# A new issue order for the output projection and the experts of a diffusion block; all normed rows stay on chip for the router

## The chip, the cores and the metric

The kernel runs on one core of a Trainium2 chip. The metric is the device time of one execution in microseconds; a time is told as the median of several executions. Durations and waits come from one profiled execution.

## The reference

One layer of a diffusion block, 1024 latent tokens and 256 context tokens of width 1024, all in float32:

```python
h = rmsnorm(x, g_mix[l]) * (1.0 + sc1) + sh1
hc = rmsnorm(xc, g_mix[l]) * (1.0 + csc1) + csh1
y, y_c = token_mixers(h, hc, w_in[l], w_out[l], ...)     # three head groups, then concat @ w_out
x = x + gt1 * y
h2 = rmsnorm(x, g_ffn[l]) * (1.0 + sc2) + sh2
x = x + gt2 * hier_moe(h2, w_rg[l], b_rg[l], w_re[l], b_re[l], w_gate[l], w_up[l], w_down[l])
...
return rmsnorm(x, g_final)

def hier_moe(h, ...):        # 4 groups of 4 experts: best group, best 2 experts in it
    ...
    for e in range(N_EXPERTS):
        he = jax.nn.silu(t @ w_gate[e]) * (t @ w_up[e])
        y = y + gates[:, e:e + 1] * (he @ w_down[e]).astype(jnp.float32)
```

There are 16 experts with matrices of 1024 x 512, 1024 x 512 and 512 x 1024.

## The kernel before, in words

Up to about 590 us the kernel computes the input projections and the three head groups. The change leaves that part as it is. What follows, the output projection, the router, the experts and the last norm, is one list of steps (`Plan`), each with its engine, a planned duration, what it reads and writes, and a sort key. A list scheduler goes through a model of the engines and queues and takes, among the steps that are ready, the one of smallest key, where `SHIFT2` adds a number to the key of each kind of step. `emit` then issues the instructions in that order, and each engine works through its own in that order. So the tables of numbers decide the order on every engine, and the instructions themselves stay the same. An instruction that waits holds up all that stands behind it on its engine.

Precision: every float32 weight slab of 128 x 512 (256 KB) is split into a high and a low part. `slab` issues the load on SP (L1029) into one of seven places (the names R, late_vcB, kv and kc), ACT writes the high part (L1049), and DVE, for some slabs POOL, writes the low part (L1026) into a ring of 31 places (W, WX and late_ names). A product on PE is three matmuls of 512 columns (L1062, L1063, L1064).

The output projection goes over eight tiles of 128 tokens with 16 products each, 128 in all. Behind the two halves of a tile stand on DVE the gated residual (L1145, L1147), then the norm (L1163) and the shift (L1166). The normed rows go to DRAM (h2d, L1167), from where the experts gather them. The router of a tile transposes the normed rows (L1068, step `ot`), forms the logits of 4 groups and 16 experts (L1184, `ol`), finds group, two experts, gates and slots in some thirty small steps on DVE (from L1191 on: groups, choose from L1203 on, base L1221, gates, slots), and writes two entries for each token into a table in DRAM by an indirect DMA of POOL (L1247). For the tiles named in `AGAIN` the transposes read the normed rows from a copy that SP reads back from h2d (L1029 into a tile F), in place of the rows that DVE has written:

```python
H2 = Hn
if t in AGAIN:
    H2 = ("F", "h2", t)
    k += LAGR
    load(1.39, (k, "hr"), lambda: buf(H2), lambda: h2d[rows], [H2], r=[("h2d", t)],
         after=[chain["lg", t - 1]] if t else [])
```

A matmul with ones (L1281) counts the tokens of each expert three times: over the first two tiles (it names the first expert), over the first six (`rank_experts`, L1296 to L1308, orders the others by their count, into `oi`), and over all eight. The 16 experts, in the order of their count, are worked through in 23 blocks (numbers 0 to 22) of 128 or 64 table rows. The first expert has block 0 (128 rows) and 1 (64), which hold tokens of tiles 0 to 5 alone, and block 2, which needs all tiles. Blocks 20, 21 and 22 are those of the last three experts, block 3 that of the second. For a block SP loads the table's rows (L1426 into IX), POOL gathers the tokens (L1429), PE transposes them into one of two buffers T (L1444), ACT takes the high part (L1456) and DVE the low one (L1460); such a buffer is free when both have read it. Then come 8 gate, 8 up and 8 down products, and POOL adds the result, times a gate (L1491), to the sum in DRAM (L1432). The last expert's block takes the sum back itself (L1568) and writes its rows of the output, beside the last norm of all tiles (`final_tile`, from L1588 on). The 15 experts behind the first bring 15 x 24 = 360 slabs.

## Time and profile before

| | |
|---|---|
| median of 3 executions | 1187.8 us (1187.21 to 1189.05) |
| profiled execution | 1187.43 us |
| its span in the trace | 1185.7 us |
| mean granted clock of PE, as a share of full speed | 0.953 |
| PE busy | 1051.8 us (89%) |
| DVE busy | 914.1 us (77%) |
| ACT busy | 723.3 us (61%) |
| POOL busy | 415.5 us (35%) |
| read from and written to DRAM | 168.95 MB and 24.07 MB |

PE is TensorE, DVE VectorE, ACT ScalarE, POOL GpSimd; SP is the engine that issues most transfers. Busy time leaves out the issuing of DMAs. The execution took 1.7 us more than the span of its trace.

### The profile page before, as it was taken

Reading aid. Unit: us, or ns where it says so; the run is one execution under the profiler, and the core shown is the slowest. Engines: PE = TensorE matmul, PEld = TensorE weight load, DVE = VectorE, ACT = ScalarE, POOL = GpSimd, SP = SyncE. Lnnn points to the kernel's source line nnn. Section 1 sums busy time; section 2 is a strip of 40 time slices with the busy share of each in tenths; the row PEclk is TensorE's granted clock in tenths of the full one; section 3 lists DMA queues with packets and bytes.
Section 4 is the critical chain, followed back from the end, with each engine's and each line's share of the span. In section 5 each row is a group of like instructions: output and inputs, shape, how many; then the busy total and the mean of one; then the engine's idle time right before and its main releaser. Section 6 shows DMA issues by size and latency. Waiting matters only on the chain. (4 is left out here: it accounts for less than half of the span.)

```text
span 1185.7 us, 18611 instructions
## 1 busy us (share of the span) xinstructions
PE 1051.8 (89%) x5620; PEld 834.4 (70%) x5620; DVE 914.1 (77%) x1742; ACT 723.3 (61%) x1451; POOL 415.5 (35%) x451
## 2 busy tenths in 40 slices
PE   5899999987999999999889986898999999999680
PEld 1688677766888888888667875676767767676560
DVE  6765779747788787788667778879787878888875
ACT  7774122218888988888732332377676667667763
POOL 0200000102778687876613444312212313222220
PEclk9899999998999999999989896799999999999895
DMA  8624674010000000000054673589999999899995
GB/s 309 228 86 145 201 234 153 10 38 11 19 1 19 1 2 19 10 1 11 13 186 150 194 225 122 163 268 280 273 295 283 293 288 285 254 284 283 277 319 226
DMA packets 99980, 191.30 MB, mean 161 GB/s; under 512 B 17720, under 2 KB 19560, under 8 KB 99750
## 3 DMA queue, kind: packets, MB, share of 16 engines
q1 hardware_dynamic: 93606, 172.59, 44.0%
q0 software_dynamic: 6272, 17.51, 6.6%
q8 instruction: 45, 0.74, 0.3%
q14 instruction: 57, 0.47, 0.1%
HBM read 168.95 MB, written 24.07 MB: 163 GB/s over the span
## 5 line engine op out<-in xcount | busy, mean ns | idle before, releaser
L685 DVE TENSOR_REDUCE st<-SC 128x1 f32<-128x1280 f32 x64 | 95.2, 1487 | 21.2 <-PE SC L680 16.3
L417 PE MATMUL acc<-wh,hH 128*128 128x512 f32 x256 | 101.3, 397 | 2.7 <-ACT bu L517 1.4
L418 PE MATMUL acc<-wl,hH 128*128 128x512 f32 x256 | 101.6, 398 | 0.0
L419 PE MATMUL acc<-wh,hL 128*128 128x512 f32 x256 | 100.8, 394 | 0.0
L1062 PE MATMUL A<-W,XP 128*128 128x512 f32 x236 | 98.3, 416 | 0.0
L1063 PE MATMUL A<-W,XP 128*128 128x512 f32 x236 | 95.4, 404 | 1.6 <-DVE W L1026 1.6
L688 ACT ACTIVATE P<-SC,st 128x1280 f32<-128x1280 f32 x64 | 85.1, 1330 | 17.0 <-DVE st L685 15.8
L1064 PE MATMUL A<-W,XP 128*128 128x512 f32 x236 | 95.0, 403 | 0.0
L1049 ACT ACTIVATE W<-R 128x512 fp32r<-128x512 f32 x111 | 68.9, 626 | 27.3 <-DMA R<-in_w_out_dram 6.4
L1026 DVE TENSOR_TENSOR W<-R,W 128x512 fp32r<-128x512 f32 x102 | 69.3, 690 | 17.9 <-ACT W L1049 15.9
L620 ACT ACTIVATE PT<-T 128x512 f32<-128x512 f32 (+1 forms) x126 | 65.1, 545 | 11.4 <-PE T L616 8.0
L732 PE MATMUL T<-vc,PT 128*128 128x64 f32 x512 | 62.2, 275 | 0.3
L1432 POOL DMA_INDIRECT accd<-F,IX x18 | 30.6, 1700 | 89.2 <-DVE F L1491 35.8
L732 PEld LDWEIGHTS T<-vc,PT 128*128 128x128 f32 x512 | 59.7, 192 | 0.7 <-ACT PT L620 0.4
L417 PEld LDWEIGHTS acc<-wh,hH 128*128 128x128 f32 x256 | 48.4, 189 | 14.2 <-issue 2.5
L680 PE MATMUL SC<-KC,QC 128*128 128x512 f32 (+1 forms) x192 | 52.4, 381 | 6.7 <-ACT P L688 6.3
L419 PEld LDWEIGHTS acc<-wh,hL 128*128 128x128 f32 x256 | 48.5, 189 | 11.4 <-issue 1.0
L418 PEld LDWEIGHTS acc<-wl,hH 128*128 128x128 f32 x256 | 48.4, 189 | 10.5 <-issue 0.7
L844 DVE TENSOR_REDUCE ast<-SA 128x1 f32<-128x640 f32 (+1 forms) x64 | 50.2, 785 | 6.5 <-PE SA L837 5.8
L442 DVE SCALAR_TENSOR_TENSOR macc<-mw,cs,macc 128x512 f32<-128x512 f32 x56 | 41.8, 747 | 17.2 <-DMA mw<-in_w_ada_dram 16.6
L1063 PEld LDWEIGHTS A<-W,XP 128*128 128x128 f32 x236 | 46.1, 195 | 11.6 <-DVE W L1026 2.4
L1062 PEld LDWEIGHTS A<-W,XP 128*128 128x128 f32 x236 | 45.9, 194 | 11.2 <-ACT W L1049 0.3
(768 smaller groups left out, 3165.4 us busy)
## 6 DMA issues: line engine op xcount, KB each, us to landing
R<-in_w_gate_dram SPq DMA_DIRECT2D x74, 256.0 KB
R<-in_w_down_dram SPq DMA_DIRECT2D x73, 256.0 KB
R<-in_w_up_dram SPq DMA_DIRECT2D x72, 256.0 KB
mw<-in_w_ada_dram SPq DMA_DIRECT2D x64, 256.0 KB
wr<-in_w_in_dram SPq DMA_DIRECT2D x32, 256.0 KB
kc<-in_w_up_dram SPq DMA_DIRECT2D x20, 256.0 KB
kc<-in_w_down_dram SPq DMA_DIRECT2D x19, 256.0 KB
late_vcB<-in_w_gate_dram SPq DMA_DIRECT2D x18, 256.0 KB
```

Source lines behind the costliest of these rows:

```text
L417: nc.tensor.matmul(acc[:, n0:n1], lhsT=a, rhs=W[k][0][:, n0:n1], start=(k == 0), stop=False)
L418: nc.tensor.matmul(acc[:, n0:n1], lhsT=a, rhs=W[k][1][:, n0:n1], start=False, stop=False)
L419: nc.tensor.matmul(acc[:, n0:n1], lhsT=b, rhs=W[k][0][:, n0:n1], start=False, stop=(k == KD - 1))
L620: nc.scalar.activation(dst, src, AF.Copy)
L685: nc.vector.tensor_reduce(small[0][:, j:j + 1], buf(("SC", u, j))[:, 0:1280], axis=AX.X, op=OP.max, negate=True)
L688: nc.scalar.activation(buf(("P%d" % j, u)), buf(("SC", u, j))[:, 0:1280], AF.Exp, bias=small[0][:, j:j + 1], accum_out=small[0][:, 2 + j:3 ...
L732: nc.tensor.matmul(buf(O)[:, 0:64], lhsT=buf(("PT", u, g))[:, (c - c0) * 128:(c - c0 + 1) * 128], rhs=vc[c // 8][:, c % 8, h * 64:(h + 1) ...
L1026: (nc.gpsimd if engine == "POOL" else nc.vector).tensor_sub(dst, a, b)
L1049: h = add("ACT", 0.525, (key, "sh"), lambda: nc.scalar.activation(buf(value)[:, 0:512], raw(), AF.Copy), r=r, w=[value], after=[chain["spl ...
L1062: nc.tensor.matmul(acc, lhsT=ah, rhs=w[:, 0:512], start=first, stop=False)
L1063: nc.tensor.matmul(acc, lhsT=ah, rhs=w[:, 512:1024], start=False, stop=False)
L1064: nc.tensor.matmul(acc, lhsT=al, rhs=w[:, 0:512], start=False, stop=last)
```

## The change

`AGAIN` is empty, so the transposes of tiles 0, 3 and 4 read the rows that DVE wrote, and three loads of 512 KB go. All shifts of the scheduler and their weight are new, and its planned durations are a little longer for products, transposes and slab loads and shorter for gathers and scatters. The number of matmuls is the same. The diff, cut to its core:

```diff
-SHIFT2 = dict(weight=0.005541, c=-100.3, fa=-315.5, fh=20.8, fl=78.4, fn=-1857.9, fo=545.6, fr=-845.7, fs=276.2,
+SHIFT2 = dict(weight=0.002103, c=-8803.8, fa=2162.2, fh=30.9, fl=130.5, fn=-2704.5, fo=-2557.1, fr=-4246.9, fs=742.6,
...
-AGAIN, LAGR = (0, 3, 4), 8.8
+AGAIN, LAGR = (), 8.8
...
-            chain["load"] = load(0.685, (key, "ld"), lambda: buf(R), src, [R], r,
+            chain["load"] = load(0.77, (key, "ld"), lambda: buf(R), src, [R], r,
...
-                    add("PE", 0.684, (b + 5.2 * n + 0.65 * k, "o"), lambda n=n, k=k, acc=acc: three(
+                    add("PE", 0.7, (b + 5.2 * n + 0.65 * k, "o"), lambda n=n, k=k, acc=acc: three(
...
-                add("PE", 0.36, (k, "ot"), ...
+                add("PE", 0.4, (k, "ot"), ...
...
-                ... w=[XG], dma=(m * 0.0164, 2.6, 2.1),
+                ... w=[XG], dma=(m * 0.0156, 2.6, 2.1),
...
-            us = 0.456 if half else 0.684
+            us = 0.466 if half else 0.7
...
-                    ... w=["sum"], dma=(m * 0.0258, 2.6, 2.7))
+                    ... w=["sum"], dma=(m * 0.0234, 2.6, 2.7))
```

What the order does at three places, as the programs have it. First, PE around the end of the output projection. Before, the last product of the projection is followed by the transposes (L1068) and logits (L1184) of tiles 6 and 7 and by the places of tile 5 (L1225, L1226), and the weights for the count over six tiles (L1281) are loaded behind them:

```order
L1064 MATMUL A_5685<-W_5684,XP_5666 128x512
L1068 MATMUL T_5692<-ident,F_5653 128x128 x4
L1068 MATMUL T_5691<-ident,F_5653 128x128 x4
L1225 LDWEIGHTS tri
L1225 MATMUL A_5687<-sel,tri 128x16
L1226 LDWEIGHTS ones
L1226 MATMUL A_5687<-sel,ones 128x16
L1184 MATMUL A_5688<-wr,kc 128x20 x8
L1068 MATMUL T_5692<-ident,F_5654 128x128 x4
L1068 MATMUL T_5691<-ident,F_5654 128x128 x4
L1184 MATMUL A_5690<-wr,kc 128x20 x8
L1281 LDWEIGHTS ones
```

After, the same count stands between two projection products (W are weight slabs, XP the token tile's two parts, A the accumulators):

```order
L1062 MATMUL A_5686<-W_5677,XP_5666 128x512
L1063 MATMUL A_5686<-W_5677,XP_5666 128x512
L1064 MATMUL A_5686<-W_5677,XP_5666 128x512
L1281 LDWEIGHTS ones
L1281 MATMUL A_5689<-selb,ones 128x16
L1225 LDWEIGHTS tri
L1225 MATMUL A_5687<-sel,tri 128x16
L1226 LDWEIGHTS ones
L1226 MATMUL A_5687<-sel,ones 128x16
L1062 MATMUL A_5690<-W_5672,XP_5666 128x512
L1063 MATMUL A_5690<-W_5672,XP_5666 128x512
```

From there 12 of the 128 projection products are still to come, of which this piece shows the first; before, all 128 stood ahead of the count. On DVE the ranking moves with it, ahead of the residual of tile 7; the low part for block 0 (L1460) now stands behind the small steps of tiles 6 and 7.

Second, SP's index loads. Before, nine of them (IX, L1426) follow the first nine slab loads of the second expert (the first rows here are the last two of these); five slab loads, eight index loads, and later the last four come behind them:

```order
L1029 ISA
L1029 DMA R_5663<-in_w_gate_dram 128x512
L1029 ISA
L1029 DMA kc<-in_w_up_dram 128x512
L1426 ISA
L1426 DMA IX_5631<-table 128x2
L1426 ISA
L1426 DMA IX_5632<-table 128x2
L1405 TENSOR_LOAD oi
L1426 ISA
L1426 DMA IX_5633<-table 64x2
L1405 TENSOR_LOAD oi
```

After, ten slab loads of that expert lie ahead, the first two of them ahead of block 0's index load, and all 21 index loads of blocks 2 to 22 follow one another before the second expert's third up slab:

```order
L1029 DMA R_5663<-in_w_gate_dram 128x512
L1029 ISA
L1029 DMA late_vcB<-in_w_up_dram 128x512
L1029 ISA
L1029 DMA R_5662<-in_w_up_dram 128x512
L1426 ISA
L1426 DMA IX_5631<-table 128x2
L1426 ISA
L1426 DMA IX_5632<-table 128x2
L1405 TENSOR_LOAD oi
L1426 ISA
L1426 DMA IX_5633<-table 64x2
```

Third, DVE near the end. Before, the low half of block 21's second transposes (XP<-T, L1460) stands behind 28 splits (L1026), the last five of them of gate slabs of block 21's own expert (late_yc<-late_vcB is the first), and a gate product (L1491):

```order
L1026 TENSOR_TENSOR late_yc<-late_vcB,late_yc 128x512
L1026 TENSOR_TENSOR WX_5657<-R_5661,WX_5657 128x512
L1026 TENSOR_TENSOR W_5670<-R_5660,W_5670 128x512
L1026 TENSOR_TENSOR late_bu<-R_5663,late_bu 128x512
L1026 TENSOR_TENSOR W_5679<-kc,W_5679 128x512
L1491 TENSOR_TENSOR F_5656<-A_5686,C_5664 128x512
L1460 TENSOR_TENSOR XP_5666<-T_5691,XP_5666 128x512
L1026 TENSOR_TENSOR late_shared<-R_5662,late_shared 128x512
```

After, both halves of block 21 stand close together, among splits of the gate slabs of the expert ahead, which is block 20's:

```order
L1026 TENSOR_TENSOR late_shared<-late_vcB,late_shared 128x512
L1026 TENSOR_TENSOR late_qc<-kc,late_qc 128x512
L1460 TENSOR_TENSOR XP_5666<-T_5691,XP_5666 128x512
L1488 SCALAR_TENSOR_TENSOR he_5668<-A_5687,IX_5648,he_5668 128x512
L1460 TENSOR_TENSOR XP_5666<-T_5692,XP_5666 128x512
L1026 TENSOR_TENSOR W_5672<-R_5663,W_5672 128x512
L1460 TENSOR_TENSOR late_qc<-T_5691,late_qc 128x512
L1026 TENSOR_TENSOR late_bu<-R_5660,late_bu 128x512
```

The second half moved ahead of all splits of its own expert's slabs, and ahead of most of those of the expert before. On PE, in the order before, 60 products stood between these transposes of block 21 and the next ones into the same buffer T. For block 13 the opposite happens: its second low half, before right behind the first, now stands behind twelve splits of its own expert's gate and up slabs, with 47 products between its transposes and those of block 15, the next into its buffer.

## Rows read from the trace of the kernel before

**Rows 1.** The page: span, busy time of each engine, and of the 40 slices of the span the busy share of PE in tenths.

```profile
span 1185.7 us, 18611 instructions
PE 1051.8 (89%) x5620; PEld 834.4 (70%) x5620; DVE 914.1 (77%) x1742; ACT 723.3 (61%) x1451; POOL 415.5 (35%) x451
...
PE   5899999987999999999889986898999999999680
```

**Rows 2.** Windows: start and end, length, then busy us and number of instructions of PE, PE's weight loads, DVE, ACT and POOL; granted clock of PE, share of the DMA engines, GB/s.

```profile
719.00:746.00 27.00, 12.87 (x60) 12.20 (x61) 19.94 (x66) 5.94 (x16) 7.61 (x11) 0.56 0.50 158
746.00:1146.00 400.00, 369.64 (x1688) 279.38 (x1687) 332.57 (x552) 267.17 (x471) 108.46 (x81) 0.97 0.89 272
780.00:1146.00 366.00, 336.38 (x1537) 253.96 (x1535) 302.08 (x461) 252.29 (x445) 96.89 (x67) 0.98 0.92 282
1146.00:1186.00 40.00, 8.21 (x26) 4.42 (x24) 20.84 (x36) 18.90 (x42) 3.06 (x3) 0.62 0.67 259
...
1160.00:1170.00 10.00, 2.02 (x3) 0.79 (x3) 8.59 (x19) 5.92 (x19) 0.00 (x0) 0.50 0.99 396
```

**Rows 3.** Timeline of PE around the end of the output projection: start, length, engine, line, operation, tiles; in brackets what it had waited for and how long.

```profile
608.19 0.39 PE L1062 MATMUL A<-W,XP 128*128 128x512 f32 x1
...
608.87 0.39 PE L1062 MATMUL A<-W,XP 128*128 128x512 f32 x1
...
691.01 0.39 PE L1064 MATMUL A<-W,XP 128*128 128x512 f32 x1
694.41 0.66 PE L1068 MATMUL T<-ident,F 128*128 128x128 f32 x4 [3.02 <-DMA F<-h2d]
...
698.10 0.83 PE L1068 MATMUL T<-ident,kc 128*128 128x128 f32 x4
...
700.53 0.64 PE L1068 MATMUL T<-ident,kc 128*128 128x128 f32 x4
700.92 0.48 PE L1062 MATMUL A<-W,XP 128*128 128x512 f32 x1
...
718.53 0.39 PE L1064 MATMUL A<-W,XP 128*128 128x512 f32 x1
722.64 1.94 PE L1068 MATMUL T<-ident,F 128*128 128x128 f32 x8 [3.73 <-DVE F L1166]
...
735.34 0.18 PE L1281 MATMUL A<-selb,ones 128*128 128x16 bf16 x1
742.97 1.97 PE L1444 MATMUL T<-ident,F 128*128 128x128 f32 x8 [7.46 <-DMA F<-h2d,IX]
...
746.22 0.77 PE L1062 MATMUL A<-WX,XP 128*128 128x512 f32 x1
```

**Rows 4.** Timeline of DVE over the router: the first and last step of a tile's groups (a small one and a half residual), the first step of a choice and what followed it, norm and shift of a tile, the last step of the ranking, and the low half for block 0.

```profile
684.49 0.17 DVE L1191 TENSOR_TENSOR lgs<-A,rb 128x20 f32<-128x20 f32 x1
685.60 0.69 DVE L1145 TENSOR_TENSOR A<-A,C 128x512 f32<-128x512 f32 x1
...
688.26 0.17 DVE L1203 TENSOR_TENSOR t<-lgs,og 128x16 f32<-128x16 f32 x1
...
691.97 1.28 DVE L1163 SCALAR_TENSOR_TENSOR kc<-F,hst,kv 128x1024 f32<-128x1024 f32 x1
...
719.96 1.28 DVE L1163 SCALAR_TENSOR_TENSOR F<-F,hst,kv 128x1024 f32<-128x1024 f32 x1
721.27 1.23 DVE L1166 TENSOR_TENSOR F<-F,kv 128x1024 f32<-128x1024 f32 x1
...
739.65 0.17 DVE L1308 CAST oi<-order 128x16 int32<-128x16 f32 x1
744.75 0.69 DVE L1460 TENSOR_TENSOR XP<-T,XP 128x512 fp32r<-128x512 f32 x1 [4.93 <-ACT XP L1456]
```

**Rows 5.** Timeline of SP and POOL, as they issue transfers: the copy read back from h2d, index loads, slab loads (the first of the second expert, its seventh up slab, the last of all), table entries, and the gather of block 0.

```profile
690.40 0.33 SPq L1029 DMA_DIRECT2D F<-h2d  x1
...
736.04 1.15 SPq L1426 DMA_DIRECT2D IX<-table  x2
740.42 0.35 SPq L1029 DMA_DIRECT2D R<-in_w_gate_dram  x1
...
757.80 6.62 SPq L1426 DMA_DIRECT2D IX<-table  x9
...
770.62 6.67 SPq L1426 DMA_DIRECT2D IX<-table  x8
777.55 0.36 SPq L1029 DMA_DIRECT2D R<-in_w_up_dram  x1
...
1155.93 0.34 SPq L1029 DMA_DIRECT2D kc<-in_w_down_dram  x1
...
738.53 1.10 POOL L1429 DMA_INDIRECT F<-h2d,IX  x1 [7.51 <-issue]
755.66 0.96 POOL L1247 DMA_INDIRECT table<-ent,sli  x1 [0.21 <-issue]
```

**Rows 6.** Timelines of PE, DVE and SP before 1106.66, and from the waits of PE from 740 to 1160 the row of its transposes: engine, tile, line, what it waited for: us in sum, times, longest.

```profile
1106.66 1.12 PE L1444 MATMUL T<-ident,kc 128*128 128x128 f32 x4 [8.04 <-DVE XP L1460]
...
1101.79 0.69 DVE L1026 TENSOR_TENSOR late_yc<-late_vcB,late_yc 128x512 fp32r<-128x512 f32 x1 [0.43 <-ACT late_yc L1049]
1105.91 0.69 DVE L1460 TENSOR_TENSOR XP<-T,XP 128x512 fp32r<-128x512 f32 x1
...
1096.79 0.33 SPq L1029 DMA_DIRECT2D late_vcB<-in_w_gate_dram  x1
...
PE T L1444 <- DVE XP L1460: 20.1, 15, 8.0
```

**Rows 7.** Timelines of PE, DVE and POOL over the end.

```profile
1165.64 0.79 PE L1062 MATMUL A<-late_bu,WX 128*128 128x512 f32 x1 [12.19 <-ACT late_bu L1049]
...
1154.49 0.16 DVE L1591 RECIPROCAL bst<-bst 128x1 f32<-128x1 f32 x1 [3.35 <-ACT bst L1113]
1161.95 0.68 DVE L1491 TENSOR_TENSOR kc<-A,C 128x512 f32<-128x512 f32 x1
...
1169.28 0.68 DVE L1491 TENSOR_TENSOR kc<-A,C 128x512 f32<-128x512 f32 x1
1170.00 1.23 DVE L1568 TENSOR_TENSOR F<-F,kc 128x1024 f32<-128x1024 f32 x1
...
1174.53 0.98 POOL L1432 DMA_INDIRECT out_dram<-kc,IX  x1 [2.00 <-DVEq L1677]
```

More of the change, by code (lines that the diff above doesn't have):

```diff
@@ L1175, in out_tile @@
                 T = ("T", "h", t, a)
-                add("PE", 0.36, (k, "ot"), lambda a=a, T=T: turn(T, lambda i: buf(H2)[:, (a * 4 + i) * 128:(a * 4 + i + 1) * 128], 4),
+                add("PE", 0.4, (k, "ot"), lambda a=a, T=T: turn(T, lambda i: buf(H2)[:, (a * 4 + i) * 128:(a * 4 + i + 1) * 128], 4),
                     r=[H2], w=[T])
@@ L1508, in expert_block @@
             add("POOL", 1.1, (k0 - 9, "xg"), lambda: B.gather(buf(XG), h2d, CUT * 128 if early else SEQ),
-                r=[("IX", j)] + [("h2d", t) for t in range(CUT if early else NT)], w=[XG], dma=(m * 0.0164, 2.6, 2.1),
+                r=[("IX", j)] + [("h2d", t) for t in range(CUT if early else NT)], w=[XG], dma=(m * 0.0156, 2.6, 2.1),
                 after=[chain["x", j - 2]] if j > 1 else [])
@@ L1514, in expert_block @@
                 k = k0 - 2 + a * 0.5
-                chain["x", j] = add("PE", 0.36 + 0.28 * half, (k, "xt"), lambda a=a, T=T: B.turn(buf(T), buf(XG), a * nt, nt), r=[XG], w=[T])
+                chain["x", j] = add("PE", 0.39 + 0.28 * half, (k, "xt"), lambda a=a, T=T: B.turn(buf(T), buf(XG), a * nt, nt), r=[XG], w=[T])
                 add("ACT", 0.48, (k, "xh"), lambda a=a, T=T: B.high(buf(XP), 8, buf(T), a * nt, nt), r=[T], w=[XP])
                 add("DVE", 0.6, (k, "xl"), lambda a=a, T=T: B.low(buf(XP), 8, buf(T), a * nt, nt), r=[T], w=[XP])
-            us = 0.456 if half else 0.684
+            us = 0.466 if half else 0.7
             for x, name in enumerate("gu"):
@@ L1535, in expert_block @@
             k = key(15) + 2
-            add("PE", 0.36, (k, "ht"), lambda: B.turn(buf(T), buf(HE), 0, 4), r=[HE], w=[T])
+            add("PE", 0.4, (k, "ht"), lambda: B.turn(buf(T), buf(HE), 0, 4), r=[HE], w=[T])
             add("ACT", 0.3 if half else 0.48, (k, "hh"), lambda: B.high(buf(HP), 4, buf(T), 0, 4), r=[T], w=[HP])
@@ L1554, in expert_block @@
                 add("POOL", 1.75, (kd, "ys"), lambda: B.scatter(accd[:, :], buf(YE), compute_op=OP.add),
-                    r=[YE, ("IX", j)] + [("acc", t) for t in range(NT)], w=["sum"], dma=(m * 0.0258, 2.6, 2.7))
+                    r=[YE, ("IX", j)] + [("acc", t) for t in range(NT)], w=["sum"], dma=(m * 0.0234, 2.6, 2.7))
                 return
@@ L1566, in expert_block @@
             chain["late"].append(j)
-            add("POOL", 1.1, (kd - 12, "xa"), lambda: B.gather(buf(XA), accd), r=["sum", ("IX", j)] + before, w=[XA], dma=(m * 0.0164, 2.6, 2.1))
+            add("POOL", 1.1, (kd - 12, "xa"), lambda: B.gather(buf(XA), accd), r=["sum", ("IX", j)] + before, w=[XA], dma=(m * 0.0156, 2.6, 2.1))
             add("DVE", 1.15, (kd, "fa"), lambda: nc.vector.tensor_add(buf(XA)[:m], buf(XA)[:m], buf(YE)[:m]), w=[XA, YE], port=True)
```

12 lines of the change are left out of this document (6 added, 6 removed).

## The prediction, made before the changed kernel ran

> **What bounds the kernel now.** I read the page's busy line and slices first [rows 1]: PE is busy for 1051.8 of 1185.7 us, and its slices stand at 9 except in a few; the reader is to look for those few. Windows over the last stage then show where they lie [rows 2]. The expert stage (746 to 1146) keeps PE busy for 369.64 of 400 us at a granted clock of 0.97, with the DMA engines at 0.89; no order can win much more than the 30.4 us that PE is idle there. From 719 to 746, between the last output projection product and the first expert product, PE is busy for 12.87 of 27 us at a clock of 0.56, and from 1146 on for 8.21 of 40. The change can only win time in these gaps, as it removes no matmul. So I followed each gap back with the timelines of PE, DVE and SP.
>
> **The gap at the start.** The timeline of PE [rows 3] shows two losses. At 694.41 it has waited 3.02 us for a tile's normed rows, which were read back from DRAM; behind that wait the work of 694.41 to 698.10 (two products and two groups of four transposes) takes 3.69 us, where at full clock a product takes 0.68 us (608.19 to 608.87) and four transposes 0.39 (700.53 to 700.92), together 2.14. That is 1.55 us for the lower clock. The second loss begins with the last projection product at 718.53: transposes and logits of tiles 6 and 7 follow, and only behind them, at 735.34, the one matmul that counts the tokens of each expert over tiles 0 to 5. On DVE the ranking ends at 739.65 [rows 4], behind it the first index load issued at 736.04, the gather at 738.53 [rows 5], the transposes at 742.97, the low half of their result at 744.75, and the first expert product at 746.22.
>
> In the new order the count stands ahead of the last 12 projection products (front part of this document). Twelve products are 12 x 0.68 = 8.2 us, so count, ranking and index load run beside them: from the count at 735.34 to the transposes at 742.97 it takes 7.6 us before. That branch is then ready at about the end of the projection, which I call X. What is late next is DVE, since the low half for block 0 now stands there behind the whole router of tiles 6 and 7. I add it up from X, with a small step taken as 0.17 us and a large one of 512 columns as 0.69 (a split, or half of a residual sum) [rows 4, 6]:
> - two residual steps 1.4, gates of tile 5 0.5, four splits 2.8, norm and shift of tile 7 1.28 + 1.23: 7.2;
> - tile 6: groups (684.49 to its end 1.1 later), choice 3.7 (688.26 to 691.97), base, slots and gates ten small steps, 1.7: 6.5;
> - four splits 2.8;
> - tile 7: 1.1 + 3.7, base and slots 1.0: 5.8;
> - the low half 0.69.
>
> That is 23.0 us. PE needs less beside it: transposes of tile 7 can start at X + 7.2 and take 2 us, its logits 3.6. X itself moves from 718.9 to about 714, by the 3.0 + 1.55 us above, as the reloads of tiles 0, 3 and 4 and their waits go; I bound it by 718.9 (another wait takes the place) and 710 (the loss of clock around tiles 3 and 4 counted twice). The first product then starts at 714 + 23 = 737 where it was 746.22: **-9.2 us**, bounds -4.3 and -13.2.
>
> On the reload a page of the Trainium skill has a price as well: "DMA: Bandwidth & Descriptors", section "Anatomy of one DMA", puts a transfer at 2.0 us plus its bytes at 436 GB/s, which is an estimate of 3.2 us for these 512 KB (the page measured it on the path of GpSimd). The trace has 4.0 us from the issue at 690.40 to the transposes that waited, so here it took longer; by the page's figure the wait, and the sum, would be 0.8 us smaller.
>
> **Do the transfers follow?** The second expert's weights must come earlier too, or PE gains a start and loses it at block 3. Before, SP issues the index loads as nine (6.62 us), some weight loads, then eight (6.67 us), and the load of the second expert's seventh up slab at 777.55 [rows 5]. The new order issues 21 of them in one row, 21 x 0.735 = 15.4 us, ahead of its third up slab. The first of these needs tile 7's table entries, which before are written at 755.66. By the sum above the slots of tile 7 are known at X + 22.3 = 736, two entries of 1 us each and 2.1 us until an index load can go (755.66 to 757.80 before) put the row at 740 to 756, ahead of where SP stood before. Its cover is that ten slabs of the second expert lie in the ring ahead of it, and that no place for more is free until block 2 has used the first expert's slabs. Cost: 0; if the entries come after 758, up to 7 us.
>
> **The stall at 1106.** The waits of PE from 740 to 1160 name one large one: 8.04 us at 1106.66 for DVE's low half of block 21 [rows 6]. DVE had it at 1105.91, since ahead of it stood splits of gate slabs of block 21's own expert; the first, at 1101.79, is of a slab that SP issued only at 1096.79. PE stood at a transpose for block 22, whose buffer still held that half. In the new order both low halves of block 21 stand ahead of these splits. PE would have done useful work until block 21 needs these slabs, and they arrive no earlier: the first is split at 1102.5, against the restart at 1106.66. I take the difference, -4.2, and 0.3 for the clock: **-4.5 us**. Bounds 0 (the slabs bind) and -11.1 (8.04 and 3.1 of lower clock, an estimate: twice the 1.55 us that followed the wait of 3.02 at 694.41).
>
> **The tail.** It is a chain of fixed links [rows 7]: the last product waits 12.19 us for the last slab until 1165.64, then 1169.28 the gate product, 1170.00 the sum, 1174.53 the last indirect write. In the new order the gate product of the last block's first half (now 1161.95) comes ahead of a final-tile step that waits 3.35 us, and the last split comes a little earlier. **-1**, bounds 0 and -2.
>
> **Sum.** Other edits (planned costs 0.684 to 0.70 and so on) change no instruction, only the order, which is counted above. -9.2 - 4.5 - 1 = -14.7. The profiled execution took 1187.43 us for a span of 1185.7; the median of the runs is 1187.8, so 0.4 above it. 1187.4 - 14.7 is **1172.7 us**. With all terms at their good bounds it is 1187.4 - 13.2 - 11.1 - 2 = 1161.1, with all at their bad ones 1187.4 - 4.3 = 1183.1.
>
> **The rivals.**
> 1. *The start is won, and lost again to the transfers.* For it speaks the DMA share of 0.92 from 780 to 1146 [rows 2], and SP's long row of index loads. Against it: the tail moves 396 GB/s where the stage moves 282, so the queues have room. It leaves about half of the start, and the stall's cause moves with the slabs: -3 to -10, about 1180.
> 2. *Nothing changes at the end.* The weights, in sequence, set the end (the last load waits for the ring in both), and earlier starts only lengthen PE's waits: within 0.2%, 2.4 us, which is about what a measurement of this kernel can tell from no change.
> 3. *Slower: the stall comes back at other blocks.* In the new order the second low half of block 13 stands on DVE behind twelve splits of its own expert's slabs (before: behind none), and the next transposes into its buffer, block 15's, follow on PE after 47 products. At 1106 it was 28 splits and 60 products. PE waits 15 times for such a half now, 20.1 us in sum, of which one is 8.0 [rows 6]. One more of that size is 8.04 + 3.1 = 11.1 us and takes most of the gain (1184); two make it slower, -14.7 + 22.2 = +7.5, 1195 us. It decides if the new waits on these low halves exceed 14.7 us. Against it: 47 products are 32 us, in which twelve slabs come at the pace of the stage (360 slabs in the 415 us from 740 to 1156, 1.15 each), so that 14 us do.
> 4. *More than I sum.* The stage has 30.4 us of idle PE; 8.0 of it is the stall, and if the new order closes half of the other 22 too, the time is 1172.7 - 11 = 1161 or less.
>
> **How the numbers follow.** My case (-10 to -21, 1166 to 1177) 0.47; more than that 0.07; rival 1 (1177 to 1185) 0.24; rival 2, within 2.4 us, 0.08; rival 3 0.14. That makes 0.78 for faster, 0.08 for the same, 0.14 for slower. The range goes from 1161 to 1187: below it lies part of the case of more (0.05), above it rival 3 and little of rival 2.
>
> **What would show it.** In the profile after: no load into a tile of normed rows from h2d on SP, PE without the wait of 3 us near 692; the last projection product near 714; the count matmul among projection products; the first expert product near 737; the row of 21 index loads on SP before 760; no wait of 8 us of PE for DVE at a transpose; last product near 1151. I am wrong if PE's waits from 740 to 1150 are greater than before, or if the first expert product comes later than 743: then tile 7's router, which I put wholly behind X, costs more than 23 us.

## The result, and the profile of the changed kernel

The changed kernel takes 1201.7 us in the median (1192.2 to 1203.2), beside 1187.8 us for the kernel before. The ratio is 1.0108, 95% interval 1.0076 to 1.0140: about 13 us slower, where I had forecast 14.7 us faster. A second set of runs of the same kernel gave 1.0087 (1.0063 to 1.0111), so 10 to 13 us.

The page answers to [rows 1]: PE is busy 6.7 us longer, the span is 15.3 us longer (the traced execution took 1203.2 us).

```profile
span 1201.0 us, 18583 instructions
PE 1058.5 (88%) x5620; PEld 837.1 (70%) x5620; DVE 914.7 (76%) x1742; ACT 719.5 (60%) x1451; POOL 416.3 (35%) x451
...
PE   5899989978999999999899885989989989989880
```

The windows answer to [rows 2], with the same columns.

```profile
719.00:746.00 27.00, 12.04 (x58) 10.73 (x57) 20.80 (x72) 7.52 (x20) 9.11 (x13) 0.59 0.74 213
746.00:1146.00 400.00, 361.94 (x1640) 273.01 (x1639) 318.16 (x515) 255.51 (x455) 102.73 (x73) 0.96 0.85 258
780.00:1146.00 366.00, 329.13 (x1488) 247.39 (x1489) 295.64 (x451) 242.00 (x434) 95.20 (x64) 0.97 0.88 270
1146.00:1186.00 40.00, 21.91 (x79) 13.54 (x77) 30.49 (x51) 26.90 (x54) 6.99 (x5) 0.82 0.97 343
```

The reader is to see that the gap at the start has not closed, and that the expert stage moves less: 258 GB/s where it moved 272, and 48 matmuls fewer between 746 and 1146. What was not done there is done behind 1146. PE falls behind mostly from 860 to 1090. From 860 to 980 and from 980 to 1090, first before, then in the changed kernel, then in h_start (the old order up to the first expert product, see the experiments):

```profile
860.00:980.00 120.00, 112.99 (x521) 85.81 (x520) 96.96 (x151) 84.28 (x151) 31.63 (x23) 0.99 0.92 290
980.00:1090.00 110.00, 103.12 (x483) 76.64 (x482) 92.70 (x145) 75.55 (x136) 29.71 (x21) 1.00 0.91 273
```

```profile
860.00:980.00 120.00, 107.35 (x491) 80.30 (x490) 89.99 (x139) 77.15 (x139) 32.97 (x21) 0.99 0.86 264
980.00:1090.00 110.00, 100.31 (x445) 75.00 (x445) 91.05 (x140) 73.11 (x133) 27.11 (x19) 0.94 0.89 274
```

```profile
860.00:980.00 120.00, 109.63 (x498) 83.00 (x497) 95.58 (x150) 76.75 (x139) 33.78 (x21) 0.97 0.88 270
980.00:1090.00 110.00, 99.25 (x449) 73.71 (x448) 90.48 (x139) 76.43 (x138) 30.16 (x21) 0.95 0.90 277
```

The changed kernel does 68 matmuls fewer in these 230 us (and 23 fewer from 780 to 860), h_start 57 fewer. From 1090 to 1146 they do more than the kernel before (232 and 231 beside 190), which waits there for 8 us at its stall.

Timeline of PE over the end of the projection [rows 3]. The wait of 3.02 us for a reload is gone; two waits on DVE stand there instead, and the last projection product starts at 719.35, before at 718.53.

```profile
681.39 0.66 PE L1068 MATMUL T<-ident,F 128*128 128x128 f32 x4 [3.30 <-DVE F L1166]
698.98 0.17 PE L1226 MATMUL A<-sel,ones 128*128 128x16 bf16 x1 [2.14 <-DVE sel L1221]
711.23 0.17 PE L1281 MATMUL A<-selb,ones 128*128 128x16 bf16 x1 [0.66 <-DVE selb L1280]
...
719.35 0.39 PE L1064 MATMUL A<-W,XP 128*128 128x512 f32 x1
745.20 1.11 PE L1444 MATMUL T<-ident,F 128*128 128x128 f32 x4 [8.50 <-DMA F<-h2d,IX]
748.93 0.79 PE L1062 MATMUL A<-WX,XP 128*128 128x512 f32 x1
```

The count stands where the order put it (711.23, before 735.34), the ranking is done at 715.86 (before 739.65), and still the first expert product comes 2.7 us later. DVE, POOL and SP show what it waited for [rows 4, 5]:

```profile
715.86 0.17 DVE L1308 CAST oi<-order 128x16 int32<-128x16 f32 x1
726.24 1.04 POOL L1247 DMA_INDIRECT table<-ent,sli  x1 [0.19 <-DVE W L1026]
727.58 2.02 POOL L1247 DMA_INDIRECT table<-ent,sli  x1 [0.21 <-issue]
734.40 1.15 SPq L1426 DMA_DIRECT2D IX<-table  x2
735.59 0.57 SPq L1156 DMA_DIRECT2D accd<-F  x1
736.29 0.35 SPq L1167 DMA_DIRECT2D h2d<-F  x1
737.01 1.05 POOL L1429 DMA_INDIRECT F<-h2d,IX  x1 [7.31 <-DMA IX<-table]
...
755.11 17.58 SPq L1426 DMA_DIRECT2D IX<-table  x21
772.96 0.33 SPq L1029 DMA_DIRECT2D R<-in_w_up_dram  x1
...
1173.04 0.34 SPq L1029 DMA_DIRECT2D R<-in_w_down_dram  x1
```

The index load of blocks 0 and 1 goes at 734.40, 18.5 us after the ranking. What it waited for are the two table entries of tile 5, written from 726.24 on. The gather behind it takes 8.2 us to the transposes (737.01 to 745.20), where it took 4.4 before (738.53 to 742.97); two stores of tile 7 go just ahead of it, at 735.59 and 736.29, and slab loads beside it. The row of 21 index loads holds SP for 17.58 us, and SP issues no slab in that time. The last slab load is at 1173.04, before at 1155.93.

Waits of PE for DVE at its transposes, from 590 to 1200 (in us: sum, times, longest), and the longest of the second row with its releaser. They answer to [rows 6]: the wait of 8.04 us is gone; the second row stood at 4.8 us in 5 waits before.

```profile
PE T L1444 <- DVE XP L1460: 15.9, 13, 3.0
PE T L1444 <- DVE he L1488: 10.7, 8, 5.0
784.37 1.12 PE L1444 MATMUL T<-ident,he 128*128 128x128 f32 x4 [4.98 <-DVE he L1488]
783.58 0.74 DVE L1488 SCALAR_TENSOR_TENSOR he<-A,IX,he 128x512 f32<-128x512 f32 x1
```

### The profile page after: what moved, and what is told of

It reads as the page before. It is cut to its first block, busy times and chain, and to the rows that moved or that the text cites. A ratio compares the mean times of both kernels' runs of the same rounds, so it can differ in the third digit from the quotient of the medians.

```text
span 1201.0 us, 18583 instructions
## 1 busy us (share of the span) xinstructions
PE 1058.5 (88%) x5620; PEld 837.1 (70%) x5620; DVE 914.7 (76%) x1742; ACT 719.5 (60%) x1451; POOL 416.3 (35%) x451
## 5 line engine op out<-in xcount | busy, mean ns | idle before, releaser
L1062 PE MATMUL A<-W,XP 128*128 128x512 f32 x230 | 96.8, 421 | 5.7 <-DVE he L1482 2.6
L1063 PE MATMUL A<-W,XP 128*128 128x512 f32 x230 | 93.6, 407 | 2.4 <-DVE W L1026 1.3
L688 ACT ACTIVATE P<-SC,st 128x1280 f32<-128x1280 f32 x64 | 85.1, 1330 | 16.8 <-DVE st L685 15.7
L1064 PE MATMUL A<-W,XP 128*128 128x512 f32 x230 | 92.6, 403 | 0.0
L1026 DVE TENSOR_TENSOR W<-R,W 128x512 fp32r<-128x512 f32 x101 | 71.2, 717 | 13.3 <-ACT W L1049 12.9
L1062 PEld LDWEIGHTS A<-W,XP 128*128 128x128 f32 x230 | 44.9, 195 | 18.5 <-ACT W L1049 3.4
L1432 POOL DMA_INDIRECT accd<-F,IX x15 | 24.5, 1633 | 80.6 <-DVE F L1491 17.3
```

Of the source, the lines that this page charges most:

```text
L688: nc.scalar.activation(buf(("P%d" % j, u)), buf(("SC", u, j))[:, 0:1280], AF.Exp, bias=small[0][:, j:j + 1], accum_out=small[0][:, 2 + j:3 ...
L1026: (nc.gpsimd if engine == "POOL" else nc.vector).tensor_sub(dst, a, b)
L1062: nc.tensor.matmul(acc, lhsT=ah, rhs=w[:, 0:512], start=first, stop=False)
L1063: nc.tensor.matmul(acc, lhsT=ah, rhs=w[:, 512:1024], start=False, stop=False)
L1064: nc.tensor.matmul(acc, lhsT=al, rhs=w[:, 0:512], start=False, stop=last)
```

## The experiments

Where a kernel only moves steps, its diff is a list of pairs: a step, named by its kind, what it writes and which of several it is, and the step that it is put ahead of (behind it where the last entry is True). The rest of the order stays word for word.

**Which half of the order costs the time.** All steps behind the head groups are issued from a list that joins the two orders at one point; a buffer keeps its place where it can.

```diff
-        for i in self.order():
+        seq = STEPS_IN_ORDER          # one order up to a chosen product, the other from there on
+        self.slot.update(PLACE_OF)
+        for i in seq:
             self.steps[i][3]()
```

> The changed kernel's instructions in the changed kernel's order up to the first expert product, and from there the order of the kernel before (its expert stage and its end). Theory (the order of the expert stage carries most of the loss, the start some 2 to 3 us): the first expert product stays at 748 to 749, and the time falls to 1.002 +- 0.002 of before, some 8 us below the changed kernel. Rival (the start carries it, and what follows only hands it on): as the changed kernel, 1.008 to 1.010.

> The opposite half: the order of the kernel before up to the first expert product (without its three reloads, since the normed rows stay on chip), and the changed kernel's order behind it, with its 21 index loads in a row and its own end. Theory: first expert product near 746, and 1.005 to 1.008 of before. Rival (the start carries the loss): 1.000 +- 0.002.

> The changed kernel's order up to the first product of block 8 (so its start, its 21 index loads in a row and its first third of the expert stage), the order of the kernel before from there on. If the row of index loads and the blocks behind it carry the loss of the stage: 1.007 to 1.010, as the changed kernel. If the loss builds up evenly over the stage: 1.004 to 1.006. If it is the last two thirds: 1.002 to 1.003.

Measured: h_end 1.0013 (0.9982 to 1.0044), h_start 1.0098 (1.0065 to 1.0132), h_mid 1.0070 (1.0039 to 1.0100). The new start with the old expert stage costs nothing that can be measured, although its first expert product comes later than in both kernels, and the old start with the new expert stage costs as much as the whole change. First expert product and last slab load, of h_end and then of h_start:

```profile
750.23 0.79 PE L1062 MATMUL A<-WX,XP 128*128 128x512 f32 x1
1156.56 0.34 SPq L1029 DMA_DIRECT2D kc<-in_w_down_dram  x1
```

```profile
743.96 0.79 PE L1062 MATMUL A<-WX,XP 128*128 128x512 f32 x1
1161.15 0.35 SPq L1029 DMA_DIRECT2D R<-in_w_down_dram  x1
```

h_end begins 4.0 us late and issues its last slab 0.6 us late; h_start begins 2.3 us early and issues it 5.2 us late. So the end follows the last slab load, not the first product. h_start's traced execution took 1190.9 us, where its median is 1196.1, so its trace shows less of the loss than the ratio does. The 340 last slab loads, counted back from the last of 384:

| | start of the last 340 | last load | between | span's end behind the last load |
|---|---|---|---|---|
| before | 781.1 | 1155.9 | 374.9 | 29.8 |
| h_end | 781.4 | 1156.6 | 375.2 | 30.2 |
| h_mid | 781.9 | 1160.8 | 378.8 | 29.3 |
| h_start | 779.6 | 1161.2 | 381.6 | 27.7 |
| changed kernel | 783.2 | 1173.0 | 389.9 | 28.0 |
| changed kernel, again | 780.4 | 1165.6 | 385.2 | 27.7 |

In the new order 340 slabs take 382 to 390 us, in the old one 375; what follows the last load takes 28 to 30 us in all six. The length alone does not tell the end: in b_best, below, the 340 begin at 773.8 and take 382.3 us, and its time stays that of before. The stream does not fall behind evenly. Beside the trace of before, the changed kernel issues its 61st slab 3.1 us late, its 229th 16.1 late (before: 979.0) and its last 17.1; h_start issues them 0.6 us early, 5.5 and 5.2 late. So the lag comes up to some 980 us and stays after that.

By the ratios, the order ahead of block 8's first product carries some 7 us of the loss (h_mid less h_end, 0.57%) and the order behind it 2 to 5 (the changed kernel's two ratios less h_mid), each known to about 5 us only. On PE the loss shows later: where h_mid's order leaves that of the changed kernel, PE starts its 4477th matmul at 879.7; before it does so at 879.6, and in the changed kernel at 882.8.

Single traces are not comparable to a few us at the start. The first projection product, ahead of which no step was moved, starts at 587.3 to 594.0 in the twenty traces; it is at 592.3 before, 592.2 in the changed kernel, 591.9 in h_end and 592.1 in h_start.

**The start by itself.**

```diff
+    (('ox', ('acc', 7), 0), ('ix', ('IX', 0), 0), False),      # a_stores: tile 7's stores ahead
+    (('ox', ('h2d', 7), 0), ('ix', ('IX', 0), 0), False),
```
```diff
+    (('r8', ('sli', 5), 0), ('k', 'oi', 0), False),            # a_entries5: tile 5's entries
+    (('r7', ('ent', 5), 0), ('k', 'oi', 0), False),            # ahead of the ranking
+    (('r9', ('tab', 5, 0), 0), ('orn', ('rs', 6), 0), True),
...
+    (('ix', ('IX', 0), 0), ('c', ('C', 'gt2'), 0), False),
+    (('ix', ('IX', 1), 0), ('c', ('C', 'gt2'), 0), False),
```

b_entries5 does the same to the kernel before (there `r5`, `r6` and `r8` of tile 5 go ahead of tile 7's residual or tile 6's shift, `r9` ahead of POOL's norm step of tile 7). b_again is the kernel before with `AGAIN = ()` alone, which gives its order anew.

> The changed kernel, with the two stores of tile 7 (512 KB each, the residual and the normed rows) moved on SP ahead of the first index load. In the changed kernel they are issued at 735.6 and 736.3, just ahead of block 0's gather at 737.0, which PE gets 8.2 us later, where it got it 4.4 us after issue before. Theory that the gather shares the queues with them: they are done before it, it lands 2 to 3 us earlier, and the first expert product moves from 748.9 to about 746.5. Rival: the six slab loads issued from 736.9 to 740 make the gather long; then it lands within 1 us of where it did. The whole time moves by at most 3 us in either case.

> The changed kernel, with tile 5's table entries moved: its slots and gates stand on DVE ahead of the ranking, its two indirect writes on POOL behind the norm step of tile 6, and the index loads of blocks 0 and 1 on SP ahead of the load of gt2. Theory that the first index load waits for tile 5's entries and not for the ranking (in the changed kernel the ranking ends at 715.9, tile 5's entries are issued at 726.2 and 727.6, and the index load goes at 734.4 after waiting for them): the index load goes at about 721, the gather is done before tile 7's logits end at 736.7, PE does not wait 8.5 us for it, and the first expert product comes at about 740 instead of 748.9. If the start carries to the end, the time falls by 5 to 9 us; if the weights' stream sets the end, by less than 3 us. Rival, the prediction's: the ranking released that load, and nothing moves.

> The kernel before, with tile 5's base, count of places and slots moved ahead of the second residual half of tile 7 on DVE and of the last projection products on PE, its two table writes ahead of tile 7's norm step on POOL, and the index loads of blocks 0 and 1 ahead of the load of gfin on SP. Theory that this wait, and not the ranking, sets the first expert product: the index load goes at about 725 instead of 736, PE no longer waits 7.5 us for the gather, and the first product comes 3 to 5 us earlier (the low half for block 0 still stands behind the ranking on DVE, which then waits for the count). The time falls by 2 to 5 us if a start carries to the end. Rival: the slabs set the end, and the time stays within 2.4 us.

> The kernel before with AGAIN empty and nothing else: its shifts, weight and planned costs stay, and the planner finds the order anew, since the three loads and their places are gone. The prediction's term: PE's wait of 3.0 us at 694 and 1.55 us of lower clock go, and the last projection product comes 4 to 5 us earlier. Rival, from the changed kernel's trace: the transposes wait for DVE's normed rows in place of the reload (3.3 us at 681, 2.1 at 699), and the last projection product stays within 1 us of where it was. What the new order does in the expert stage is open: shifts that were found for another graph may fit worse, so that the whole time may grow by 10 us or more.

Measured: a_stores 1.0086 (1.0054 to 1.0119), a_entries5 1.0076 (1.0047 to 1.0104), b_entries5 0.9977 (0.9950 to 1.0004), b_again 1.0168 (1.0128 to 1.0207). With the stores ahead the gather takes 5.6 us from its issue to the transposes (lines 17 further down), where it took 8.2, and the first expert product comes at 746.39, as the theory had it:

```profile
737.06 1.05 POOL L1446 DMA_INDIRECT F<-h2d,IX  x1 [8.84 <-DMA IX<-table]
742.65 1.12 PE L1461 MATMUL T<-ident,F 128*128 128x128 f32 x4 [7.43 <-DMA F<-h2d,IX]
```

So, by this one trace, the stores carry most of the 3.8 us by which the gather is longer than before. PE's wait falls only from 8.5 to 7.4 us, as the gather itself is issued no earlier. With the entries ahead the first expert product comes at 744.32 in the changed kernel, not at the 740 expected, since PE then waits 3.09 us for a selection of tile 7 at 741.50; in the kernel before it comes at 741.77, and the wait of 7.46 us is halved:

```profile
738.52 1.97 PE L1444 MATMUL T<-ident,F 128*128 128x128 f32 x8 [3.68 <-DMA F<-h2d,IX]
```

So tile 5's entries were what block 0 waited for. In b_entries5 the last slab load comes 2.5 us earlier, but its projection begins 2.3 us earlier too, so the trace does not show this as an effect of the edit.

On X two runs speak. In b_again, where the planner orders all steps anew, the last projection product does not come earlier (720.94) without the reloads. In h_start, which keeps the old order there and leaves out the reloads, it does:

```profile
710.65 0.39 PE L1064 MATMUL A<-W,XP 128*128 128x512 f32 x1
```

From the first projection product to the last it takes 118.6 us there. In four traces of the old order with the reloads (before, b_low21, b_xtight, b_row) it takes 122.3 to 127.4, in the changed kernel 127.2, in b_again 128.8. So in the old order the term is there, some 4 to 9 us by one trace; in the new order other waits take its place.

b_again also goes against the rule that the end follows the last slab load: it issues that load 4.2 us earlier than before and ends 18 us later. Its loads of the sum for the last norm, which stand ahead of the last slab load in both kernels, come behind it, and the end is 52 us behind the last slab load:

```profile
1151.74 0.34 SPq L1029 DMA_DIRECT2D R<-in_w_down_dram  x1
1166.13 0.33 SPq L1029 DMA_DIRECT2D kc<-accd  x1
```

**The index loads in a row.** a_spread puts each index load of blocks 6 to 22 eight slab loads ahead of its gather; b_row gathers those of blocks 11 to 22 into one row in the kernel before; b_best is b_entries5 with those of blocks 7 to 22 spread.

```diff
+    (('ix', ('IX', 7), 0), ('ld', ('R', 'W', 13, 'g', 5), 0), False),     # a_spread
+    (('ix', ('IX', 8), 0), ('ld', ('R', 'W', 13, 'd', 1), 0), False),
...
+    (('ix', ('IX', 11), 0), ('xt', 'extra', 0), False),                   # b_row
+    (('ix', ('IX', 12), 0), ('xt', 'extra', 0), False),
```

> The changed kernel, with the index loads of blocks 6 to 22 moved on SP, each to eight slab loads ahead of the place of its gather; those of blocks 2 to 5 stay. Theory that the row of 21 index loads costs time: it holds SP from 755.1 to 772.7, the second expert's third up slab is issued at 773 and DVE and ACT are late with its splits, so PE waits 5.0 us at 784 and loses about 4 more to the clock. Then the slab load is issued before 762, the wait of 5 us goes, and the span falls by 5 to 9 us. Rival, the prediction's: the row is hidden because the ring has no free place anyway; then the loads go no earlier and the time stays within 2.4 us.

> The kernel before, with its index loads of blocks 11 to 22 moved forward so that all 21 stand in one row on SP, ahead of five slab loads. It is the same question asked from the other side. If the row costs time, the second expert's second up slab is issued at about 758 + 17.6 = 775 instead of 766, PE waits near 780 to 790, and the time grows by 5 to 9 us (1193 to 1197). If the row is hidden, the time stays within 2.4 us of before.

> The kernel before with both findings: tile 5's table entries and the first two index loads early (the run that gave 0.9977), and the index loads of blocks 7 to 22 no longer in rows on SyncE but each eight slab loads ahead of its gather. Theory (index rows cost the slab stream time): 0.995 to 0.9975 of before, 2 to 3 us below the run without the spreading. Rival (in this order the shorter rows are covered): 0.9975 to 0.998, no better than that run.

Measured: a_spread 1.0076 (1.0038 to 1.0114), b_row 1.0027 (1.0002 to 1.0052), b_best 0.9984 (0.9955 to 1.0013). In the kernel before the longer row brings the changed kernel's wait with it, with the same releaser (this kernel's lines are 27 further down):

```profile
777.66 0.69 PE L1471 MATMUL T<-ident,he 64*128 64x64 f32 x4 [4.43 <-DVE he L1515]
```

b_row shows the row's price as 0.3%, some 3 us, just clear of the noise and below the 5 to 9 expected. a_spread's wait falls from 4.98 to 1.42 us (another of 2.70 follows), but its time, 0.1 to 0.3% below the changed kernel's two, is not clear of them by itself. Shorter rows bring nothing in the old order (b_best): there the rival holds.

**The stall at 1106.** In the kernel before both halves of block 21's second group of transposes go ahead of the splits of expert 12's gate slabs:

```diff
+    (('xh', ('XP', 'x', 21), 1), ('sh', ('W', 12, 'g', 0)), False),
+    (('xl', ('XP', 'x', 21), 1), ('sl', ('W', 12, 'g', 0)), False),
```

> The kernel before, with two steps moved: the high part of block 21's second transposes on ACT and the low part on DVE stand ahead of the splits of that block's own gate slabs, where they stood behind five of them. It measures the stall of 8.04 us at 1106 by itself. The prediction's term: the wait goes, the time falls by about 4.5 us (1183), and the slabs of block 21 bind next. Rival: the wait with the lower clock behind it was all lost, as the progress of products in the changed kernel says (40 products' matmuls that took 22.3 us there take 11.2 in it): -8 to -11 us (1177 to 1180). Third: the time only moves to the wait for the last slab in the tail, which grows from 12.2 to about 20 us, and the end stays where it was (within 2.4 us).

Measured: 1.0003 (0.9975 to 1.0031). The wait of 8.04 us is 2.36 (lines 17 further down), and PE stands a little later, now for a slab:

```profile
1102.12 0.66 PE L1461 MATMUL T<-ident,kc 128*128 128x128 f32 x4 [2.36 <-DVE XP L1477]
...
1108.03 0.79 PE L1079 MATMUL A<-W,XP 128*128 128x512 f32 x1 [4.43 <-ACT W L1066]
```

The slab loads stay within some 2 us of where they were. The largest single wait of PE in the stage is worth nothing that can be measured; the interval leaves a gain of at most 3 us.

**Which wait in the new expert stage.** Four candidates. b_xtight moves low halves of blocks close behind their high halves in the kernel before, as the new order has them; a_xlate moves 24 of them two splits later in the changed kernel; a_yg moves the products with the gate (L1491) ahead of up to three splits; a_he3 keeps the order and gives the tile `he` a third place.

```diff
+    (('xl', ('XP', 'x', 3), 0), ('sl', ('W', 9, 'u', 0), 0), False),      # b_xtight
+    (('xl', ('XP', 'x', 3), 1), ('sl', ('W', 9, 'u', 5), 0), True),       # a_xlate
+    (('yg', ('F', 'ye', 0), 0), ('sl', ('W', 8, 'g', 1), 0), False),      # a_yg
...
-NW, NR, NF, NH = 19, 4, 4, 2
+NW, NR, NF, NH = 19, 4, 4, 3
```

> The kernel before, with 15 low halves of gathered tokens moved on DVE ahead of the one weight split that stands between them and their high half, which is how the changed kernel has them. If low halves right behind their high halves slow the stream of slabs, DVE waits for ACT there as in the changed kernel (some 8 to 15 us where it was 2.2), and the time grows by 3 to 8 us. Rival: such waits lie beside other waits, and the time stays within 2.4 us of before.

> The changed kernel, with 24 low halves of gathered tokens (blocks 3 to 22) moved on DVE behind the next one or two weight splits. In the changed kernel DVE waits for ACT's high half at 16 of them, 16.3 us in sum from 790 to 1146 (before: 2.2 us), since each stands right behind it; meanwhile the splits behind it, and so the loads that wait for a free place, stand. Theory that this slows the stream of slabs: the wait falls to 3 us or less, the last slab load goes out earlier by 5 to 10 us than 1173, and the time falls by as much. Rival: PE, which waits for the same low halves (15.9 us, 13 times), waits longer for them by as much, and the time stays within 2.4 us.

> The changed kernel, with 39 of the products with the gate row gt2 (L1491) moved on DVE ahead of up to three weight splits. In the changed kernel ACT waits 19.2 us, 9 times, at its fold (L1479) for a buffer that these products hold (before: 6.0 us, 4 times, in the same window 790 to 1146), with the high parts of slabs queued behind it. Theory that this slows the stream of slabs: the wait falls below 6 us, the last slab load goes out 5 to 10 us earlier, and the time falls by as much. Rival: the products are not ready that early, as PE is not done with them, so DVE waits for PE instead, with the splits behind it, and the time stays or grows.

> The changed kernel in its own order, nothing moved, with three places instead of two for the hidden layer's rows (the tile he). The waits ACT he L1479 <- DVE kc and <- DVE F L1491 (9.9 and 9.3 us in 780 to 1150, at most 2.6 of them in the kernel before) are for such a place, and the slab splits queue behind them on ACT. Theory (these waits slow the slab stream): both waits fall under 4 us together, the last slab load comes 3 to 6 us earlier than in the changed kernel, and the time falls to 1.003 to 1.006 of before. Rival (the waits are filled by other waits on ACT, as when the fold-in was moved): the waits go, the time stays at 1.008 to 1.011.

Measured: b_xtight 1.0033 (1.0003 to 1.0064), a_xlate 1.0103 (1.0064 to 1.0142), a_yg 1.0179 (1.0138 to 1.0220), a_he3 1.0114 (1.0081 to 1.0147). The three edits of the changed kernel took away the waits that they aimed at, and the time did not fall; a_yg is slower than the changed kernel. b_xtight adds waits to the kernel before, some 4 us of DVE for XP (2.2 to 6.7), and its time grows by 0.3%, just clear of the noise like b_row's: such waits may cost some 4 us in the old order, though a_xlate, which takes 16.8 us of them away (18.7 to 1.9), gives nothing back in the new one. Largest waits of ACT from 780 to 1150 in the changed kernel, then in a_he3:

```profile
ACT he L1479 <- DVE kc L1491: 9.9, 4, 3.1
ACT he L1479 <- DVE F L1491: 9.3, 5, 2.3
```

```profile
ACT he L1485 <- PE A L1064: 21.6, 7, 7.6
ACT W L1049 <- DMA R<-in_w_gate_dram: 9.5, 7, 2.5
```

The 19.2 us of waits for a place of `he` (6.0 in the kernel before) are gone, and ACT waits for PE and for slabs instead; its last slab load is at 1165.9, as in the changed kernel's second run. My theory of these two waits fell here, as that of the low halves did in a_xlate and that of the gate products in a_yg.

**What can be mended together.** a_comb is a_entries5, a_spread and earlier stores in one; after_2 is the changed kernel again, beside it on the same chip.

> The changed kernel with three of the edits tried one by one put together: tile 5's entries and the first index loads earlier (alone 1.0076 of before), the index loads of blocks 6 to 22 spread (alone 1.0076), the two stores of tile 7 ahead of the second expert's first loads (a like move alone 1.0086), where the changed kernel itself had 1.0108. Theory that the changed kernel lost its time at the start and in the row of index loads: the parts add up to -0.32 - 0.32 - 0.22 = -0.86 per cent, and the ratio is about 1.002. Rival: each part only moves a wait along, the order of the expert stage itself is slower, and the ratio stays at 1.007 or above.

> The changed kernel itself, once more, beside the three that follow, since it and the kernels derived from it have been compared with the kernel before at different times. All theories: a ratio of 1.008 to 1.014 to the kernel before.

Measured: a_comb 1.0048 (1.0026 to 1.0071), after_2 1.0087 (1.0063 to 1.0111). In a_comb the gather is out of the way, and what is late next is the router of tiles 6 and 7, which I had predicted for the changed kernel itself:

```profile
739.20 1.11 PE L1444 MATMUL T<-ident,F 128*128 128x128 f32 x4 [0.48 <-DMA F<-h2d,IX]
742.76 0.17 PE L1225 MATMUL A<-sel,tri 128*128 128x16 bf16 x1 [2.44 <-DVE sel L1218]
```

The first expert product comes at 745.57, and half of the loss is left: the time lies between the theory (1.002) and its rival (1.007 and above).

**The places of the slabs.** b_r8 is b_entries5 in the same order, with an eighth place for slabs on their way in:

```diff
-NW, NR, NF, NH = 19, 4, 4, 2
+NW, NR, NF, NH = 19, 5, 4, 2
```

> The kernel before with tile 5's entries early (the run that gave 0.9977) and eight places instead of seven for slabs on their way in, order unchanged. Theory (the slab stream, limited by how soon its places come free, sets the end): the waits of SyncE's queue for split slabs shrink, the last slab load comes 3 to 10 us earlier, and the time falls to 0.985 to 0.994 of before. Rival (the transfer engines are full, at a share of 0.92): the eighth place only makes each load longer, and the time stays at 0.996 to 0.999.

Measured: 0.9888 (0.9848 to 0.9928), 1170.9 us beside 1182.8, the only kernel that is clearly faster than both. Its page, its expert stage, its first expert product and its last slab load:

```profile
span 1167.7 us, 18609 instructions
780.00:1146.00 366.00, 334.75 (x1516) 254.15 (x1515) 307.71 (x473) 255.59 (x463) 99.08 (x66) 0.97 0.93 293
736.71 0.77 PE L1062 MATMUL A<-WX,XP 128*128 128x512 f32 x1
1138.28 0.34 SPq L1029 DMA_DIRECT2D R<-in_w_down_dram  x1
```

The eighth place by itself is worth 0.9% (0.9888 beside b_entries5's 0.9977, each known to 0.3 or 0.4). The last 340 slabs start at 771.3, in b_entries5 at 777.9, and take 367.0 us in place of 375.5. The rival, full transfer engines, is refuted: the stage moves 293 GB/s where it moved 282. The places are one limit among others, as one place more in seven gives a stream only 2.3% faster. One part of the expectation failed: SP's waits for split slabs hardly shrink (145.7 us from 780 to 1150, in b_entries5 150.0).

## Why the prediction was wrong

**The frame.** I summed gaps of PE and let each microsecond of them arrive at the end. h_start and h_end show that a shift of the first expert product by 2 to 4 us does not, and b_low21 that the longest wait of the stage does not either. The end is the last slab load and some 28 to 30 us in both kernels. The loads follow each other through seven places, and b_r8 shows, in the old order, that these are a limit on them. My rivals 1 and 2 named this; rival 2 even had the reason (the last load waits for the ring), and I gave the two 0.32. The order of the expert stage had no term of its own in my sum beside the stall, the index loads and the tail; h_start shows that the loss of 10 to 13 us lies in the order behind the first expert product.

**The start, -9.2.** Two steps failed. *X moves to 714*: it stayed at 719.35, by the bound that I had named, another wait in the place of the removed one (3.30 us for a tile's normed rows, 2.14 for a selection). h_start shows that the reloads did cost something in the old order (710.65), so it is the new order that takes this back. *Count, ranking and index load as one branch that the count releases*: the index load of blocks 0 and 1 needs the first expert, known after two tiles, and tile 5's entries, but not the ranking. The rows of before said so: it was issued at 736.04, and the ranking ended at 739.65 [rows 4, 5]. An instruction that goes before another has ended did not wait for it. The list of 23 us behind X was never tested by the changed kernel, as it waited for the gather; a_comb shows its end, 745.57, 26 us behind its last projection product at 719.38. My sign of being wrong, a first expert product later than 743, thus came (748.93), but not for the reason that I gave, tile 7's router. The other sign came too: PE's waits from 740 to 1150 are 46 us (42 in the second trace), before 40.

**The transfers, 0 (to 7).** The row of 21 loads went at 755.11, later than the 740 of my sum but before the 758 up to which I called it harmless, and took 17.58 us instead of 15.4. The cover that I named, ten slabs in the ring ahead of it, was too short: PE waited 4.98 us at 784.37 for a step behind late splits. b_row gives 3 us for it, h_mid less h_end 7 us together with the blocks up to 8. The worth lies between the value that I took and the upper bound. I had also left that bound out of the sum of the bad ones, which is 1190.1 with it and not 1183.1.

**The stall at 1106, -4.5.** The mechanism held and the wait went; its worth is the lower bound, 0 (b_low21), since the slabs bind: PE's next wait there is 4.43 us for a slab's split.

**The tail, -1.** From the last slab load to the end of the span it is 28.0 us, before 29.8: within its bounds, in one trace of each.

**The rivals.** Slower came true, to which I had given 0.14, but not by rival 3's way: the waits on the low halves fell in sum, from 20.1 to 15.9 us, and no wait of 8 us came at block 15. What came is a slab stream that is slower in the new order, by 7 to 15 us over 340 slabs, with the lag there by some 980 us.

**What stays open.** Why the new order slows the stream of slabs. SP's waits for split slabs from 780 to 1150 are longer; the largest row before, and in h_start:

```profile
SPq L1029 <- DVE W L1026: 46.6, 62, 2.6
```

```profile
SPq L1029 <- DVE W L1026: 70.0, 69, 3.3
```

All rows of waits for a split (L1026, on DVE or POOL) sum to 143.5 us before (148 waits), 146.9 in h_end (132), 162.4 in h_start (160) and 163.2 in the changed kernel (145). That points to splits that end later in the new order, but it is not shown as the cause: in a_xlate the sum is down to 151.9, at an unchanged time. Three single waits in front of the splits were taken away without a gain, so it may be the order of splits and other steps on ACT and DVE as a whole, or a fourth wait; no run tells these apart, and none changes the order between 860 and 1090 alone. An eighth place in the new order was not tried.

## What to carry to other kernels

Where loads pass through a ring of places, first find out whether the ring sets their pace, by one more place: here that was worth 0.9%, more than any edit of the order gained. Then cost a change of order by what it does to the return of the places and to the queue that issues the loads, and count the waits of the compute engine only where they delay these. Before a step is taken as the releaser of another, compare the two times: what was issued before the other's end did not wait for it.

## What the runs showed of the hardware

The same gather took 4.4 us from its issue to its use in the kernel before and 8.2 us with two stores of 512 KB issued just ahead of it; with these stores issued 8 us ahead of it, it took 5.6 us (a_stores, one trace). An index load costs SP 0.84 us when many follow each other (21 in 17.58 us), and the slab loads behind them wait that long. A DMA share of 0.92 was not the limit of the transfer engines: with an eighth place for slabs (b_r8) the stage moved 293 GB/s at a share of 0.93, where it had moved 282.
